# Feed-forward operands of a Hymba-style layer: the low part of each split operand by an accumulating DMA in place of a VectorE subtraction

## The chip, the cores and the metric

The kernel runs on one core of a Trainium2 chip. The metric is the device time of one execution in microseconds (us), the median over several runs. The engines of the core are PE (TensorE), DVE (VectorE), ACT (ScalarE), POOL (GpSimd) and SP (SyncE). Transfers run on 16 DMA engines that all queues share; before the change every transfer that matters here is issued by SP.

## The reference

One post-norm layer for 1024 positions of width 1024. A mixer (state-space group, retention group, output projection) is followed by a layer norm, and then by the part that the change touches:

```python
def conv_ffn(x, w_up, conv_w, conv_b, w_down):
    ug = x @ w_up                       # 1024 x 5632
    a, g = ug[..., :D_FF], ug[..., D_FF:]          # D_FF = 2816
    a_pad = jnp.pad(a, ((0, 0), (CONV_W - 1, 0), (0, 0)))
    a = sum(conv_w[i] * a_pad[:, i:i + seq_len] for i in range(CONV_W)) + conv_b
    return (jax.nn.silu(a) * g) @ w_down           # 1024 x 1024
x = layer_norm(ALPHA * x + ffn, ln2_g, ln2_b)
```

All of it is float32.

## The kernel before

Float32 precision is had from TensorE's float32r products: each operand is split into a high part (the value rounded to float32r) and a low part (value minus high part), and a product is the sum of three matmuls: high by high, high by low, low by high. The function `split` makes the two parts of a 128x512 operand: ScalarE casts the source into the high part (line 913), VectorE subtracts it from the source into the low part (line 914). The parts stand in a ring of 10 slots (`ring`, filled in `up_setup`), reused in turn, so a slot can be filled again when the products of the operand ten splits earlier are through.

Both products of the feed-forward use Strassen-Winograd, seven block products for eight.

*Up projection* (spans from 403 to 823 us of the profile). A loop over 22 blocks f of 128 hidden units. For each f, `up_products` runs seven products of 12 matmuls (A11, S2, S3, S1, A12, A22, S4), then adds, convolution, SiLU and gate; `up_prep(f + 1)` makes the next seven operands, and `up_load(f + 3)` loads weights that far ahead. Four operands are sums made by VectorE in place in the raw weights, and three of these sums overwrite something that an earlier split still reads: line 932 writes `sS[:, 0]`, the source of the S1 split of the block before; line 934 overwrites a11, the source of the A11 split; line 941 overwrites a12, the source of the A12 split. For the first three blocks the A11 split (and for two of them A12) is made early, while the output projection and first layer norm of the mixer still run; that layer norm has steps on POOL (lines 824 and 831).

*Down projection* (823 to 1034 us). Three sweeps over 11 pairs m of hidden blocks; `down_prep` loads and splits four operands for a pair (two of `araw`, which comes back from DRAM, two of the weights `wd`). One step of a pair uses two of the splits, for 12 matmuls; a sweep has 22 such steps and the three sweeps 66. In the third sweep line 1081 overwrites b21 right after its split, and the result is split again. A last sweep takes its operands from `down_prep_last` (lines 1089 and 1090), which has a cast and a subtraction of its own and does not call `split`.

`split` is called 154 times in the up projection (22 by 7) and 132 times in the down projection (33 by 4): 286 times. The instructions of each engine run in a fixed order, which a planner sets when the kernel is built, from its own costs; each engine waits in that order.

Of the kernel before, what the change touches and what calls it, by code (L numbers as in the profile page):

```python
# [31 lines left out]
# columns of the constant pack  # L32
C_COS, C_SIN, C_MASK, C_XI, C_ZETA, C_G128, C_SGN, C_DM, C_MH, C_END = (
    0, 256, 768, 1280, 1284, 1288, 1290, 1292, 1308, 1312)
# columns of the state-space parameter pack
# [37 lines left out]
class Arena:  # L73
    """Hand-placed SBUF: slots of 8 KB a partition, reused in the order in which they are freed."""
# [32 lines left out]
def layer_kernel(ctx, tc, a, out):  # L107
# [11 lines left out]
    kept = {}       # banks that outlive a turn of the rotation  # L119
# [9 lines left out]
    def f32(t):  # L129
        return t.bitcast(F32)  # L130
# [6 lines left out]
    # ------------------------------------------------------------ inputs of the first phase  # L137
    # mixer-phase small pool
# [28 lines left out]
    def load_w(blk, kp):  # L167
        """two k-tiles of one 512-column block of w_in, split into two float32r parts"""
        n = f"wsp{blk}_{kp}"
        if blk == 1:  # L170
            load_x(kp)
        t = A.get([P, 2, 2, 512], F32R, n)
        rs = []
        for q in range(2):
            wr_n[0] += 1
            r = mp.tile([P, 512], F32, tag=f"wraw{wr_n[0] % 3}", name=f"wraw{blk}_{kp}{q}")
            SP.dma_start(r, a["w_in"][blk, :, 2 * kp + q])
            rs.append(r)
            if blk == 1:
                load_xk(2 * kp + q)  # L180
        for q, r in enumerate(rs):
            S.copy(t[:, q, 0], r)
            V.tensor_sub(t[:, q, 1], r, f32(t[:, q, 0]))
            if blk == 1:
                split_xk(2 * kp + q)
        if blk == 1:
            A.free(f"xraw{kp}")
        return t, n

    # ------------------------------------------------------------ input projection  # L190
    def project(blk, lhs, banks, between=None, after=None):
        """psum[j] (j = 0..7) += x-part.T @ w_in block, k outermost; between: small products to run among the first,
        before the last bank is begun"""
        ws = []
        for kp in range(4):
# [17 lines left out]
            if late:  # L213
                if kp == 0:
                    continue
                after()
                bank_n[0] -= 1          # the bank of the small products
                banks[7] = bank("late")
                for k in range(4):
                    wk = ws[k // 2][:, k % 2]  # L220
                    mm3(banks[7], lhs(k, 0, 7), lhs(k, 1, 7), wk[:, 0], wk[:, 1], k == 0, False)
                A.free(f"wsp{blk}_0")
# [10 lines left out]
    # products of zeros while the first loads are under way, to have the tensor engine's clock up when they arrive  # L233
# [7 lines left out]
    # ------------------------------------------------------------ q, k  # L241
# [7 lines left out]
    for b in range(8):  # L249
# [9 lines left out]
        # q carries gamma^(t+1), which the decay masks take back  # L259
# [8 lines left out]
    # ------------------------------------------------------------ u  # L268
# [17 lines left out]
    # ------------------------------------------------------------ state-space parameters  # L286
# [49 lines left out]
    # lam_bar = mag cos + i mag sin;  cos = 1 - 2 sin^2(r/2)  # L336
# [5 lines left out]
    V.scalar_tensor_tensor(nr, cm, -2.0, m1, ALU.mult, ALU.add)      # Re lam_bar - 1  # L342
# [5 lines left out]
    # kappa = (lam_bar - 1) / lam  # L348
# [16 lines left out]
    def cmul(oR, oI, aR, aI, bR, bI, n, tA=tA, tB=tB):  # L365
        """(aR + i aI) * (bR + i bI) on [P, n, 32]; b is one [P, 32] vector"""
        va = lambda t: t.rearrange("p (m g) -> p m g", g=32)
        bb = lambda t: t.unsqueeze(1).broadcast_to([P, n, 32])
        x, y = va(tA[:, :32 * n]), va(tB[:, :32 * n])
        V.tensor_mul(x, va(aR), bb(bR))  # L370
        V.tensor_mul(y, va(aI), bb(bI))
        V.tensor_sub(va(oR), x, y)
        x2, y2 = x, y
        V.tensor_mul(x2, va(aR), bb(bI))
        V.tensor_mul(y2, va(aI), bb(bR))
        V.tensor_add(va(oI), x2, y2)
# [5 lines left out]
    # kappa * Lambda^m  # L382
# [3 lines left out]
    def rev_pow(t, lo):  # L386
        """[P, 16 g, 8 j, 16 c] view of powers 7-j (stored [m, g]) for groups lo.."""
# [15 lines left out]
    # ------------------------------------------------------------ chunk inputs and kernels  # L403
# [10 lines left out]
    # powers of Lambda^8  # L414
# [9 lines left out]
    # signed imaginary parts: coefficient of the swapped copy, for out = [re; im] and its swap  # L424
# [10 lines left out]
    # chunk states V[(ri, s), 0, g, chunk], one chunk late; the second half is for states with re and im swapped  # L435
# [18 lines left out]
    # short kernels K[(7-m, c'), g, c]  # L454
# [25 lines left out]
    # ------------------------------------------------------------ scan over the chunks  # L480
    def swapped(h, j):
        """position j of every super-chunk, re and im swapped"""
# [19 lines left out]
    def scan_carries():  # L502
        # inclusive states at the end of the 16 super-chunks, carried with Lambda^64
# [18 lines left out]
    def scan_correct(car):  # L522
        # states += Lambda^(8 (j+1)) * carry of the super-chunk before
# [18 lines left out]
    # ------------------------------------------------------------ v  # L542
# [9 lines left out]
    # ------------------------------------------------------------ gate  # L552
# [4 lines left out]
    # ------------------------------------------------------------ state-space output  # L557
    # output taps CT[(ri, s), i', g, c] with Lambda^(8-i'); T'[(j, c'), i', g, c]
    UT, CT, TT = [], [], []
    # L1 = [Lr; -Lr], L2 = [-Li; -Li]  # L560
# [45 lines left out]
    # ------------------------------------------------------------ retention  # L606
# [3 lines left out]
    # heads 0, 2 (state rows 0-63) and 1, 3 (rows 64-127) keep to banks of their own  # L610
# [49 lines left out]
    def ret_norm(b):  # L660
        # per-head norm, gate
# [62 lines left out]
    def glu_setup():  # L724
        # GLU weights [P, k, 512]
# [13 lines left out]
    # one part's products fill the waits of the other  # L739
# [14 lines left out]
    # ------------------------------------------------------------ second half of the mixer  # L754
    def load_split(src, n, name, wide):
        """weights [P, 2048] per raw slot -> float32r parts [P, 2, hl, 1024]"""
# [49 lines left out]
    # Strassen-Winograd operands of the transposed x1: halves of d (rows) and of the tokens (columns).  # L806
    # xf[d half, token half] in float32; X[...] = float32r parts (hi, lo) of [P, 4 k, 512 tokens]
# [25 lines left out]
    def layer_norm_far(zz, lnv, pool, after):  # L833
        """as layer_norm for several tiles that are not waited for"""
# [37 lines left out]
    def x1_transpose(i):  # L872
# [13 lines left out]
        if i >= 4:  # L886
            b11, b21, b12, b22 = (xf[k][:, :, cs] for k in ((0, 0), (1, 0), (0, 1), (1, 1)))
            V.tensor_sub(xt3[:, :, cs], b22, b12)        # T3
            V.tensor_sub(b11, b12, b11)                  # T1
            V.tensor_sub(b12, b22, b11)                  # T2  # L890
            V.tensor_sub(b21, b21, b12)                  # -T4

    # ------------------------------------------------------------ up projection, conv, gate
# [15 lines left out]
    def split(src):  # L909
        """the two float32r parts of a [P, 512] operand"""  # L910
# [3 lines left out]
        V.tensor_sub(t[:, 1], src, f32(t[:, 0]))  # L914
# [5 lines left out]
    def up_prep(f, first=True, rest=True):  # L920
        """operands of the seven products, in the order of their use; sums in place where they can be"""
# [8 lines left out]
        if rest:  # L930
            s1 = sS[:, 0]
            V.tensor_add(s1, a21, a22)
            V.tensor_sub(a21, a11, a21)                  # S3
            V.tensor_sub(a11, s1, a11)                   # S2  # L934
# [6 lines left out]
            V.tensor_sub(a12, a12, a11)                  # S4  # L941
# [5 lines left out]
    def ahead(f):  # L947
        """how many of the products of f run before the operands of the others are there"""
# [27 lines left out]
    def up_products(f):  # L976
# [23 lines left out]
        # causal depthwise conv, slots -2, -1 hold the last two positions of the chunk before  # L1000
# [13 lines left out]
    # operands of the down projection made of h (rows: token halves, columns: even and odd f):  # L1014
    # A11, S1, S2, S3, A12, A22, S4 for every pair of f
    hd = dr.tile([NF // 2, P, 7, 512], F32, name="hd")

    def store_h(f):
# [9 lines left out]
        V.tensor_sub(a21, a11, a21)                      # S3  # L1028
# [12 lines left out]
    # ------------------------------------------------------------ down projection, second norm  # L1041
    # Strassen-Winograd again: B rows are the even and odd f of each pair, columns the halves of n
# [8 lines left out]
    def down_load(s_, m):  # L1051
        """loads of pair m for one sweep"""
# [13 lines left out]
    def down_prep(s_, m):  # L1066
        """operands of pair m for one sweep; sums of the weights in place"""
        r = down_load(s_, m)
        b11, b12, b21, b22 = wd[m][:, 0, 0], wd[m][:, 0, 1], wd[m][:, 1, 0], wd[m][:, 1, 1]
        if s_ == 0:  # L1070
            ops = [(split(r[:, 0]), split(b11))]
            V.tensor_sub(b12, b12, b11)                  # T1
            ops.append((split(r[:, 1]), split(b12)))
        elif s_ == 1:
            V.tensor_sub(b12, b22, b12)                  # T2
            ops = [(split(r[:, 0]), split(b12))]
            V.tensor_sub(b11, b12, b11)                  # T3
            ops.append((split(r[:, 1]), split(b11)))
        else:
            ops = [(split(r[:, 0]), split(b21))]  # L1080
            V.tensor_sub(b21, b21, b12)                  # -T4  # L1081
# [3 lines left out]
    def down_prep_last(m):  # L1085
        """operands of the last sweep: S4 (which came in the place of T3) and B22"""
# [49 lines left out]
    # in the order of their last use  # L1136
# [7 lines left out]
    def residual():  # L1144
        for e in range(2):
            t = A.get([P, 4, DM], F32, f"zw{e}")
            V.tensor_copy(t[:, 0, 0:1], u[:, e, 0:1])        # holds the load back until the first sweep is through
# [3 lines left out]
    def spread(s_):  # L1151
        """alpha * x1 and what the first two sweeps give, into the quarters of the output (rows: token halves)"""
# [68 lines left out]
def lay_out(i):  # L1221
    """The inputs, rearranged (no arithmetic)."""
# [43 lines left out]
```

## Time and profile before

| | |
|---|---|
| median of 3 runs | 1043.98 us (1043.65 to 1045.77) |
| profiled execution, first to last instruction (span) | 1043.1 us |
| what lies around the span, by the median | 0.9 us |
| busy: PE, DVE, ACT, POOL | 1022.4, 827.7, 455.7, 59.5 us |
| moved by DMA | 122.22 MB, mean 117 GB/s |

For the profiled execution the page gives its span; no separate device time of that one execution stands beside it. Busy time is the time in which an engine has an instruction in work. A wait is idle time of an engine put down to the instruction that released it. The granted clock is a share of TensorE's full 2.4 GHz. The DMA share is the mean busy share of the 16 DMA engines.

### The profile page before, as it was taken

To read this page: it belongs to the slowest core of one execution; us is meant where nothing else is said; L and a number is where in the kernel's file an instruction comes from. 1 tells how busy PE (TensorE), PEld (TensorE's weight loads), DVE (VectorE), ACT (ScalarE), POOL (GpSimd) and SP (SyncE) were. 2 spreads that over 40 slices of the span, in tenths; PEclk is the share of its full clock that TensorE was granted. 3 is DMA by queue.
4 is the path that set the end of the run, shared out by engine and by line. 5 is a ranking of instruction groups with operands and counts; after the bars stand their busy time and mean duration, and the time that the engine had idled before them with its cause. 6 is when DMAs were issued, how large, how long until landed. Compare 5 with 4: busy or idle time off the path is not lost.

```text
span 1043.1 us, 12923 instructions
## 1 busy us (share of the span) xinstructions
PE 1022.4 (98%) x4780; PEld 862.0 (83%) x4780; DVE 827.7 (79%) x1406; ACT 455.7 (44%) x786; POOL 59.5 (6%) x64
## 2 busy tenths in 40 slices
PE   9999999999999998999999999999999999999996
PEld 7899888887899886788888888888888888888885
DVE  5387999966855799999687787787776896749987
ACT  5121663044622255655444444444444545444710
POOL 0000000002100262000000000000000000000003
PEclk9999999999999999999999999999999999999999
DMA  8400401413500422043223233123133895743103
GB/s 287 156 1 1 172 19 43 135 67 122 184 0 23 159 82 101 13 150 140 91 108 115 79 112 142 51 111 142 51 131 126 308 321 208 256 137 125 53 37 125
DMA packets 37263, 122.22 MB, mean 117 GB/s; under 512 B 4192, under 2 KB 6624, under 8 KB 32336
## 3 DMA queue, kind: packets, MB, share of 16 engines
q1 hardware_dynamic: 36912, 120.88, 32.6%
q8 instruction: 37, 0.61, 0.3%
q10 hardware_dynamic: 288, 0.52, 0.1%
q14 instruction: 26, 0.21, 0.1%
HBM read 90.22 MB, written 31.16 MB: 116 GB/s over the span
## 4 chain that ended last, share of the span: by engine, by line
PE 86%; DVE 6%; issue 2%; POOL 2%; ACT 2%; DMA 1%; POOLq 0%; SPq 0%; DVEq 0%; ACTq 0%
PE dn L134 6%; PE dn L135 6%; PE dn L133 6%; PE u L206 4%; PE qk L206 4%; PE g L206 4%; PE wo L133 2%; PE wo L134 2%; PE wo L135 2%; PE o L634 1%; PE v L206 1%; PE o L636 1%; PE y L599 1%; POOL z L831 1%; PE glu L133 1%
## 5 line engine op out<-in xcount | busy, mean ns | idle before, releaser
L913 ACT CAST ring<-wu 128x512 fp32r<-128x512 f32 x132 | 81.4, 620 | 144.0 <-DVE wu L934 6.3
L914 DVE TENSOR_TENSOR ring<-wu,ring 128x512 fp32r<-128x512 f32 x132 | 92.8, 705 | 18.9 <-ACT ring L913 18.9
L133 PE MATMUL dn<-ring 128*128 128x512 f32 x264 | 102.7, 389 | 0.0
L134 PE MATMUL dn<-ring 128*128 128x512 f32 x264 | 102.7, 389 | 0.0
L135 PE MATMUL dn<-ring 128*128 128x512 f32 x264 | 102.7, 389 | 0.0
L913 ACT CAST ring<-araw 128x512 fp32r<-128x512 f32 x66 | 41.1, 623 | 78.2 <-PE dn L134 67.2
L914 DVE TENSOR_TENSOR ring<-araw,ring 128x512 fp32r<-128x512 f32 x66 | 45.6, 691 | 29.6 <-ACT ring L913 29.6
L133 PEld LDWEIGHTS dn<-ring 128*128 128x128 f32 x264 | 49.5, 188 | 10.4
L134 PEld LDWEIGHTS dn<-ring 128*128 128x128 f32 x264 | 49.6, 188 | 10.3
L135 PEld LDWEIGHTS dn<-ring 128*128 128x128 f32 x264 | 49.5, 188 | 10.2
L914 DVE TENSOR_TENSOR ring<-wd,ring 128x512 fp32r<-128x512 f32 x66 | 45.3, 689 | 1.0 <-ACT ring L913 1.0
L913 ACT CAST ring<-wd 128x512 fp32r<-128x512 f32 x66 | 40.7, 618 | 8.4 <-DVE wd L1081 4.4
L206 PE MATMUL u<-wsp,x 128*128 128x512 f32 x168 | 43.8, 417 | 0.0
L206 PE MATMUL v<-wsp,x 128*128 128x512 f32 x147 | 42.5, 410 | 0.4 <-ACT V L452 0.4
L206 PE MATMUL qk<-wsp,x 128*128 128x512 f32 x168 | 40.5, 403 | 1.4 <-ACT x L161 1.4
L206 PEld LDWEIGHTS u<-wsp,x 128*128 128x128 f32 x168 | 41.7, 330 | 0.1
L206 PEld LDWEIGHTS qk<-wsp,x 128*128 128x128 f32 x168 | 32.5, 194 | 9.5 <-ACT x L161 2.7
L206 PE MATMUL g<-wsp,x 128*128 128x512 f32 x168 | 38.5, 390 | 0.0
L206 PEld LDWEIGHTS g<-wsp,x 128*128 128x128 f32 x168 | 31.5, 188 | 6.9 <-ACT vt L548 0.4
L1008 DVE SCALAR_TENSOR_TENSOR cg<-Ab,cv,cg 128x1024 f32<-128x1024 f32 x22 | 28.3, 1285 | 10.6 <-ACT cg L1007 10.6
L1010 ACT ACTIVATE cg<-cg 128x1024 f32<-128x1024 f32 x22 | 23.4, 1062 | 28.8 <-DVE cg L1009 28.8
L843 POOL TENSOR_SCALAR frs<-fmv 128x4 f32<-128x4 f32 x1 | 1.1, 1147 | 604.1 <-DVE fmv L842 604.1
(1154 smaller groups left out, 2820.2 us busy)
## 6 DMA issues: line engine op xcount, KB each, us to landing
wu<-in_w_up_dram SPq DMA_DIRECT2D x22, 1024.0 KB, 5.0
araw<-hd SPq DMA_DIRECT2D x33, 512.0 KB, 3.7
wraw<-in_w_in_dram SPq DMA_DIRECT2D x32, 256.0 KB, 3.4
hd<-cg SPq DMA_DIRECT2D x22, 256.0 KB, 2.0
hd<-cg SPq DMA_DIRECT2D x11, 512.0 KB, 2.6
hd<-sS SPq DMA_DIRECT2D x11, 512.0 KB, 2.8
wd<-in_w_down_dram SPq DMA_DIRECT2D x11, 512.0 KB, 4.4
wd<-in_w_down_dram SPq DMA_DIRECT2D x22, 256.0 KB, 5.2
```

The source lines that it names most:

```text
L133: T.matmul(o, lhsT=lh, rhs=rh, start=first, stop=False)
L134: T.matmul(o, lhsT=lh, rhs=rl, start=False, stop=False)
L135: T.matmul(o, lhsT=ll, rhs=rh, start=False, stop=last)
L206: T.matmul(banks[j], lhsT=lhs(k, xi_, j), rhs=w[:, q, wi_], start=(k == 0 and xi_ == 0 and wi_ == 0), stop=False)
L599: T.matmul(o, lhsT=UT[h][:, gl], rhs=TT[h][:, :, 16 * gl:16 * gl + 16], start=True, stop=False)
L634: T.matmul(ob[h], lhsT=pt[:, e * P:(e + 1) * P], rhs=v_[:, h * P:(h + 1) * P], start=True, stop=(b == 0))
L636: T.matmul(ob[h], lhsT=qk[rows[h], h // 2], rhs=st[rows[h], h // 2], start=False, stop=True)
L831: G.tensor_add(z, z, lnv[:, 1])
L913: S.copy(t[:, 0], src)
L914: V.tensor_sub(t[:, 1], src, f32(t[:, 0]))
L1008: V.scalar_tensor_tensor(c, Af[:, P:P + 1024], cv[:, f, 1:2], c, ALU.mult, ALU.add)
L1010: S.activation(c, c, AF.Silu)
```

## The change

In `split` the VectorE subtraction is taken out. ScalarE writes the negated source, rounded in the same way, into the low part, and an adding DMA issued by GpSimd then adds the source to it in place. All other lines of the diff are comments that are taken out or blank lines.

```diff
     def split(src):
         t = ring[ring_n[0] % len(ring)]
         ring_n[0] += 1
         S.copy(t[:, 0], src)
-        V.tensor_sub(t[:, 1], src, f32(t[:, 0]))
+        S.activation(t[:, 1], src, AF.Copy, scale=-1.0)
+        G.dma_start(out=t[:, 1], in_=src, accum_op=ALU.add)
         return t[:, 0], t[:, 1]
```

Each source is 128 partitions of 512 float32: 256 KB.

## Rows read from the trace of the kernel before

**Rows 1.** The page: busy time, share of the span, number of instructions.

```profile
PE 1022.4 (98%) x4780; PEld 862.0 (83%) x4780; DVE 827.7 (79%) x1406; ACT 455.7 (44%) x786; POOL 59.5 (6%) x64
```

**Rows 2.** Windows: stretch, length, busy of each engine, granted clock, DMA share, GB/s.

```profile
core 0: us, PE busy (x) PEld busy (x) DVE busy (x) ACT busy (x) POOL busy (x), PEclk, DMA share, GB/s
350.00:400.00 50.00, 46.77 (x231) 39.04 (x229) 46.52 (x72) 21.48 (x34) 26.72 (x14) 1.00 0.20 81
...
540.00:580.00 40.00, 40.00 (x178) 33.10 (x178) 31.29 (x44) 19.39 (x34) 0.00 (x0) 1.00 0.28 99
...
823.00:883.00 60.00, 60.00 (x267) 49.67 (x266) 50.82 (x81) 28.66 (x51) 0.00 (x0) 1.00 0.77 265
883.00:943.00 60.00, 60.00 (x266) 49.71 (x265) 37.99 (x61) 26.48 (x48) 0.00 (x0) 1.00 0.57 203
943.00:1003.00 60.00, 60.00 (x266) 49.67 (x266) 56.55 (x95) 33.74 (x59) 0.00 (x0) 1.00 0.22 71
```

**Rows 3.** Waits of PE from 350 us on: in total, times, longest.

```profile
PE x1t L879 <- POOL z L831: 4.4, 1, 4.4
PE up1C L962 <- DVE ring L914: 0.6, 1, 0.6
```

**Rows 4.** Groups by line: the subtraction of split, and its cast.

```profile
L914 DVE TENSOR_TENSOR ring<-wu,ring 128x512 fp32r<-128x512 f32 x132 | 92.8, 705 | 18.9 <-ACT ring L913 18.9
L914 DVE TENSOR_TENSOR ring<-araw,ring 128x512 fp32r<-128x512 f32 x66 | 45.6, 691 | 29.6 <-ACT ring L913 29.6
L914 DVE TENSOR_TENSOR ring<-wd,ring 128x512 fp32r<-128x512 f32 x66 | 45.3, 689 | 1.0 <-ACT ring L913 1.0
...
L914 DVE TENSOR_TENSOR ring<-sS,ring 128x512 fp32r<-128x512 f32 x22 | 15.2, 692 | 0.0
...
L1089 ACT CAST last<-wd 128x512 fp32r<-128x512 f32 x22 | 12.6, 620 | 3.8 <-DVE last L1090 1.6 <-DVE zw L1159 1.6 <-DMA araw<-hd 0.3
```

**Rows 5.** Timeline of ACT, down projection, two steps of many.

```profile
889.53 0.62 ACT L913 CAST ring<-araw 128x512 fp32r<-128x512 f32 x1 [1.58 <-PE dn L134]
890.06 0.61 ACT L913 CAST ring<-wd 128x512 fp32r<-128x512 f32 x1
892.25 0.62 ACT L913 CAST ring<-araw 128x512 fp32r<-128x512 f32 x1 [1.58 <-PE dn L134]
```

**Rows 6.** Groups of ACT: the ACTIVATE of a 128x512 SBUF tile.

```profile
L1007 ACT ACTIVATE cg<-Ab,cv 128x512 f32<-128x512 f32 x19 | 15.4, 812 | 0.0
```

**Rows 7.** DMA of 823 to 1003 us: packets, MB, share of 16 engines.

```profile
q1 hardware_dynamic: 10496, 32.18, 51.9%
```

**Rows 8.** DMA issues, whole kernel: KB each, us from issue to landing.

```profile
araw<-hd SPq DMA_DIRECT2D x33, 512.0 KB, 3.7
...
hd<-cg SPq DMA_DIRECT2D x22, 256.0 KB, 2.0
hd<-cg SPq DMA_DIRECT2D x11, 512.0 KB, 2.6
```

**Rows 9.** Issuing a DMA on SP: ns min/median/max, first and last start.

```profile
L1058 SPq DMA_DIRECT2D araw<-hd x33: 319/320/434, 779.4 to 970.6; - x33
```

**Rows 10.** Groups of POOL in the first layer norm: busy, mean ns.

```profile
L831 POOL TENSOR_TENSOR z<-z,ln 128x1024 f32<-128x1024 f32 x7 | 17.3, 2476 | 8.8 <-ACT z L830 8.8
L824 POOL TENSOR_TENSOR lrsa<-lrsa,mh 128x1 f32<-128x1 f32 x8 | 12.1, 1513 | 27.4 <-DVE lrsa L823 27.4
```

**Rows 11.** Timeline of DVE, one block of the up projection.

```profile
557.92 0.69 DVE L1005 TENSOR_TENSOR Ab<-cg,up7D 128x512 f32<-128x512 f32 x1 [1.43 <-PE up7D L962]
...
562.88 0.69 DVE L932 TENSOR_TENSOR sS<-wu 128x512 f32<-128x512 f32 x1
...
566.49 0.69 DVE L941 TENSOR_TENSOR wu<-wu 128x512 f32<-128x512 f32 x1
...
572.68 0.69 DVE L934 TENSOR_TENSOR wu<-sS,wu 128x512 f32<-128x512 f32 x1
...
576.96 0.69 DVE L1005 TENSOR_TENSOR Ab<-cg,up8D 128x512 f32<-128x512 f32 x1 [1.43 <-PE up8D L962]
```

**Rows 12.** Windows around PE's one long idle time.

```profile
396.00:400.00 4.00, 0.77 (x8) 0.53 (x5) 4.00 (x6) 2.42 (x4) 2.71 (x2) 1.00 0.00 0
400.00:404.00 4.00, 2.79 (x11) 2.59 (x12) 3.18 (x6) 1.58 (x4) 1.16 (x1) 0.58 0.53 161
```

## Prediction

> **What bounds the kernel now.** I read the busy times first: PE is in work for 98% of the span, DVE for 79% [rows 1]. That is an average, so next the windows: from 540 to 580 us, and in each 60 us of the three sweeps of the down projection, PE is busy for the whole stretch at full granted clock, while DVE is busy for 31.29 of 40 us and 37.99 to 56.55 of 60 [rows 2]. Then the waits of PE from 350 us on: two, 5.0 us together, and only 0.6 us of them ended by the subtraction that goes away [rows 3]. So in the feed-forward PE sets the time, DVE's subtractions are hidden behind it, and the most that the change could win is a part of those 5.0 us. What matters is whether the new path still delivers the operands as fast as PE consumes them.
>
> PE's pace: the same DVE addition of two successive blocks starts 19.04 us apart in the up projection (557.92 and 576.96) [rows 11]: 7 products, 2.72 us each. In the down projection the casts of successive steps start 2.72 us apart, and ACT waits for PE to free a ring slot [rows 5]. One step uses two splits.
>
> **Part 1, the subtraction goes.** 286 instructions, 92.8 + 45.6 + 45.3 + 15.2 = 198.9 us of DVE [rows 4]. None of it stands on the path but for the 0.6 us above. Worth 0 to 0.6 us in the steady stages. In the early stretch (350 to 400 us) DVE is busy 46.52 of 50 us [rows 2], but five early splits' relief (five by 0.7 us) meets five DMA issues put into POOL's queue, among the layer norm steps that end PE's 4.4 us wait [rows 3]. At one POOL instruction of 1.51 us each [rows 10] that is up to 7.6 us the other way. Bounds -4.4 and +7.6; I take 0.
>
> **Part 2, ScalarE's second pass.** The negation is a 128x512 pass from SBUF to SBUF. Nearest rows: the cast, 0.62 us long and 0.53 us after the one before it [rows 5], and an ACTIVATE of that size, 0.81 us [rows 6]. Per step of the down projection ACT then has four passes: 4 by 0.53 = 2.1 us, or 2 by 0.53 + 2 by 0.71 (0.81 less the same overlap) = 2.5 us, of 2.72. It fits. Where the 22 casts of the last sweep's operands run [rows 4] in the last 15 or so steps, 1.5 more per step make 2.9 to 3.3 us: 3 to 9 us over, if nothing slower hides it. In the up projection ACT is at 19.39 of 40 us [rows 2], or 9.2 of 19.04; seven passes add 4.4 to 5.7. It fits.
>
> **Part 3, issuing on POOL.** No DMA of POOL is in the trace. Bounds: SP's issue, 0.32 us [rows 9], and POOL's longest instruction nearby, 2.48 us [rows 10]. Two per step must stay under 2.72 us, so the limit is 1.36 us each. I take POOL's shortest layer norm step, 1.51 us [rows 10], as the row of POOL's own that lies between the ends: 3.0 us per step, 0.3 over. In the up projection seven by 1.51 = 10.6 us of 19.04, and even seven by 2.48 = 17.4, fit.
>
> **Part 4, the transfers.** Each split now moves 256 KB, and adding in place means reading two operands and writing one. In 823 to 1003 us the queue moved 32.18 MB in 51.9% of 180 us [rows 7], so 256 KB of loads takes 0.76 us of all 16 engines. Stores out of SBUF are nearer to this traffic: 512 KB lands 0.6 us later than 256 KB [rows 8]. So one pass costs 0.6 to 0.76 us, and with the destination read as well, two passes, 1.2 to 1.52.
>
> The three windows of the down projection already use 0.77, 0.57 and 0.22 of 60 us each [rows 2]: 93.6 us of the DMA engines in 180. Its 132 splits add 79 us (one pass, 0.6), 100 (0.76), 158 (two passes, 1.2) or 201 (1.52). The sums are 173, 194, 252 and 294 us, against 180 of PE's. What is over 180 cannot be hidden, since loads and accumulations share the engines: 0, +14, +72 or +114 us. Each accumulation is hidden only up to (180 - 93.6) / 132 = 0.65 us. I take two passes at the store's price, 1.2 us: +72 us, a step of 252 / 66 = 3.8 us, which covers ACT's 2.1 to 3.3 and POOL's 3.0.
>
> The Trainium skill bears on the two passes: "Collectives: The Full Stack", section "The bandwidth ceiling: the fold count and why AG ≠ RS ≠ AR", says that an add inside the DMA engines costs nothing for the adding, but halves the rate because it needs two source reads. By this rule the sum is the +72 us taken; no row of this trace has an adding transfer to confirm it.
>
> In the up projection the share is 0.28 at 540 us [rows 2], and seven by 1.2 us of 19.04 add 0.44: 0.72, or 0.84 at 1.52. It fits.
>
> **Part 5, latency.** With 10 ring slots a split may begin four steps ahead in the down projection, 10.9 us. It now needs four ACT passes (2.1), an issue (1.5) and a landing of 2.0 to 3.7 us [rows 8]: 5.6 to 7.3. It fits until the landing passes 7.3 us. In the third sweep line 1081 must wait for a landing before its result is split again: two issues, two landings and 3.8 us of ACT and DVE are 10.8 to 14.2 us for five steps, 13.6; at worst 2.6 us over the sweep, and covered by the 3.8 us step. In the up projection the lead is nine products, 24.5 us. There, three sums of DVE per block (932, 934, 941) must wait until a DMA has read their source [rows 11]. Against cast and subtraction, each wait is 0.53 + 1.51 + (2.0 to 3.7) - 0.69 = 3.3 to 5.0 us longer. Behind it in DVE's order stand the additions that free PSUM banks. DVE has 31.29 of 40 us in use [rows 2], 14.9 per block, less seven by 0.7: 10.0 used, 9.0 free. The waits are 10 to 15 us if DVE stands still for all of them; as far as other instructions stand in between they cost nothing. I take 0.
>
> **Sum.** 1043.1 (the profiled span) + 72 = 1115 us, and 0.9 us around the span as in the median: 1116 us.
>
> **The rivals.**
>
> *Hidden, or faster.* If an accumulation holds the DMA engines for under 0.65 us, POOL issues in under 1.36 us and landings stay under 7.3 us, the down projection stays on PE. Then only the early stretch counts: 1038.5 to 1044 if DVE's relief comes through (up to 5.0 us). For it: one pass at the store's price is 0.6 us. Against it: the second read. The skill's page "DMA: Bandwidth & Descriptors", section "Anatomy of one DMA — SWDGE (gpsimd) path", states for a transfer from GpSimd a fixed part of about 2.0 us and the bytes at 436 GB/s, an estimate of 2.6 us for 256 KB: by that rule alone this rival would come true; SP's store of this size lands in 2.0 us [rows 8].
>
> *Mild.* One pass at the load's price (+14), or POOL's 3.0 us per step as the only limit (66 by 0.3 = +20), or ACT's 3 to 9 us in addition: 1047 to 1100.
>
> *POOL bounds.* At 2.48 us an issue, 132 issues are 327 us in 180: +147, 1191 us. It decides above 252 / 132 = 1.9 us an issue. For it: even a 128x1 instruction takes POOL 1.51 us. Against it: SP's 0.32.
>
> *VectorE bounds the up projection.* If DVE stands still for all three waits, 10 to 15 us against 9.0 free, 20 blocks lose 1 to 6 us each: 20 to 120 us beside the 72, 1136 to 1236.
>
> *The clock.* PE would wait 1.1 us in every step. After 4.4 us of idling the granted clock stood at 0.58 in one window of 4 us [rows 12]. If waits as short as these brought it to 1.2 GHz, a step would take 5.4 us: +180, 1224.
>
> **How the numbers follow.** Two passes on the DMA engines (1100 to 1160): 0.45, and it gives the predicted time. POOL, DVE or the clock above that: 0.22. Mild: 0.21. Hidden: 0.12, half faster by over 0.2%, half within it (0.2%, 2 us, is about what a measurement of this kernel tells from no change). So faster 0.06, same 0.06, slower 0.88. The range from 1047 to 1220 leaves out the hidden cases and the far end of the second group. The likeliest case's own range is 1100 to 1160.
>
> **What would show it.** DVE's busy time falls to about 629 us, ACT's rises to about 633. From 823 us on PE should be busy for some 70% of a longer stretch, its waits ended by the DMAs into the ring, with a DMA share near 1, and the up projection still at 19 us a block. If instead the DMA share stays below 0.8 while PE waits, and POOL's issues stand end to end, the issue was the limit; if DVE idles before 932, 934 or 941 and a block takes longer than 19 us, the waits were. I am wrong if PE shows no new waits.

## The result and the profile after

The changed kernel takes 1191.11 us (1187.76 to 1193.82, 4 runs), the kernel before 1044.41 us in the same comparison: a ratio of 1.1398, 95% interval 1.1383 to 1.1414. That is slower, as forecast, but by 147 us in place of 72. One execution below, the first of experiment 3 (the change without its DMA), ran at a granted clock of 0.85 from beginning to end and took 1130.8 us; its time is not compared. Experiments 1, 2 and 4 to 10 are one execution each, experiments 3 and 11 several; each is compared with the kernel before on the same chip.

The page after, its busy times and DMA queues:

```profile
PE 1062.8 (89%) x4780; PEld 874.2 (74%) x4780; DVE 653.5 (55%) x1120; ACT 595.1 (50%) x1072; POOL 304.3 (26%) x350
...
q0 software_dynamic: 41184, 74.99, 36.2%
q1 hardware_dynamic: 36912, 120.88, 28.3%
```

Against [rows 1], DVE lost 286 instructions and 174 us, ACT gained 286 and 139 us: the counts are as predicted, the times less than the 199 and 177 us that the prediction's signs go by. What sets the end is in PE: its idle time rose from 20.7 us (1043.1 - 1022.4) to 126.2 (1189.0 - 1062.8), and its busy time rose by 40.4 us for the same 4780 matmuls. Queue q0 is the new one. It held the 16 engines for 36.2% of 1189.0 us; over 286 transfers that is 1.50 us each.

The windows after, columns as in [rows 2]; the first lies in the up projection, the other three cover the down projection's three sweeps:

```profile
540.00:580.00 40.00, 37.61 (x167) 30.78 (x165) 20.06 (x27) 22.27 (x41) 11.51 (x14) 1.00 0.79 184
...
872.00:962.00 90.00, 66.06 (x255) 49.00 (x254) 25.99 (x37) 46.83 (x86) 35.31 (x42) 0.94 1.09 280
962.00:1058.00 96.00, 70.98 (x278) 53.45 (x276) 9.09 (x16) 51.10 (x95) 37.81 (x44) 0.93 1.09 270
1058.00:1147.00 89.00, 67.21 (x263) 51.86 (x263) 36.11 (x59) 55.19 (x103) 35.76 (x41) 0.92 0.89 180
```

In the sweeps the DMA share is 1.09, 1.09 and 0.89, where [rows 2] had 0.77, 0.57 and 0.22. A share above 1 means that the records count slightly more than the whole, so a price taken from it can be a few per cent too high. PE has work for about 74% of the time; POOL is busy for 40%. In the up projection nothing is full, and yet PE is no longer busy throughout.

The waits of PE after (us in total, times, longest):

```profile
PE dn L134 <- DMA ring<-wd: 68.8, 37, 9.9
PE up15D L961 <- ACT p L990: 4.9, 1, 4.9
PE up5D L961 <- ACT p L990: 3.6, 1, 3.6
PE up21D L961 <- ACT p L990: 2.7, 1, 2.7
...
PE up9D L961 <- ACT p L990: 2.4, 1, 2.4
...
PE x1t L879 <- POOL z L831: 2.3, 1, 2.3
```

So there are two new waits. In the down projection PE waits for the adding DMAs themselves. In the up projection it waits, mostly in every other block, for ScalarE's copy at line 990. (From line 915 on the lines of the changed kernel are one higher than before, and those of the runs in which `split` has a switch four higher: the sum S4 is line 941 before, 942 in the changed kernel and 945 in those runs.) The wait at `x1t`, 4.4 us in [rows 3], is down to 2.3.

From the first matmul of each stage (the starts of the groups of `up0A`, `dn<-ring` and `dn<-last` in each trace) the 145.9 us of the span come apart:

| us | before | after | difference |
|---|---|---|---|
| up to the first product of the up projection | 402.8 | 400.0 | -2.8 |
| up projection | 421.5 | 472.3 | +50.8 |
| three sweeps of the down projection | 179.5 | 275.4 | +95.9 |
| last sweep, norm, stores | 39.3 | 41.3 | +2.0 |

The issue on POOL and the landings after, first the groups of POOL (busy, mean ns), then the DMA issues (KB each, median us to landing):

```profile
L915 POOL DMA_DIRECT2D ring<-wu x132 | 115.3, 929 | 314.3 <-ACT ring L914 128.6 <-DVE cg L997 54.8 <-DVE cg L993 44.8
L915 POOL DMA_DIRECT2D ring<-araw x66 | 59.6, 903 | 106.4 <-ACT ring L914 79.3 <-DMA ring<-wd 9.4 <-DVE cg L1009 7.0
```

```profile
ring<-wu POOLq DMA_DIRECT2D x132, 256.0 KB, 4.2
...
ring<-araw POOLq DMA_DIRECT2D x66, 256.0 KB, 10.0
ring<-wd POOLq DMA_DIRECT2D x66, 256.0 KB, 9.9
```

An issue takes 0.9 us of POOL, between the bounds 0.32 and 2.48 and below the 1.51 taken; two per step fit. A landing takes 4.2 us in the up projection and 10 us in the down projection, against 2.0 to 3.7 us in [rows 8]. The 10 us is a median over two kinds: in the same view of single stretches it is 13 to 15 us in the first two sweeps, where the engines are full, and 5.0 to 5.5 us in the third.

### The profile page after: what moved, and what is told of

Its sections match the earlier page's. It is cut to its first block, busy times and chain, and to the rows that moved or that the text cites. A ratio compares the mean times of both kernels' runs of the same rounds, so it can differ in the third digit from the quotient of the medians.

```text
span 1189.0 us, 13673 instructions
## 1 busy us (share of the span) xinstructions
PE 1062.8 (89%) x4780; PEld 874.2 (74%) x4780; DVE 653.5 (55%) x1120; ACT 595.1 (50%) x1072; POOL 304.3 (26%) x350
## 3 DMA queue, kind: packets, MB, share of 16 engines
q0 software_dynamic: 41184, 74.99, 36.2%
## 4 chain that ended last, share of the span: by engine, by line
PE 34%; DMA 29%; issue 14%; DVE 9%; ACT 7%; POOL 6%; POOLq 0%; SPq 0%; DVEq 0%; ACTq 0%
DMA ring<-wu 9%; DMA ring<-wd 7%; POOL ring L915 5%; DMA ring<-araw 4%; PE u L206 4%; PE qk L206 3%; PE g L206 3%; DMA ring<-sS 3%; DMA araw<-hd 3%; ACT ring L914 2%; PE wo L133 1%; PE wo L134 1%; PE wo L135 1%; DMA wd<-in_w_down_dram 1%; PE wp L135 1%
## 5 line engine op out<-in xcount | busy, mean ns | idle before, releaser
L915 POOL DMA_DIRECT2D ring<-wu x132 | 115.3, 929 | 314.3 <-ACT ring L914 128.6
L134 PE MATMUL dn<-ring 128*128 128x512 f32 x264 | 113.2, 429 | 68.8 <-DMA ring<-wd 68.8
L134 PEld LDWEIGHTS dn<-ring 128*128 128x128 f32 x264 | 52.6, 199 | 95.2 <-DMA ring<-wd 85.0
L133 PE MATMUL dn<-ring 128*128 128x512 f32 x264 | 107.8, 408 | 1.9 <-ACT ring L913 1.5
L135 PE MATMUL dn<-ring 128*128 128x512 f32 x264 | 107.7, 408 | 0.0
L915 POOL DMA_DIRECT2D ring<-araw x66 | 59.6, 903 | 106.4 <-ACT ring L914 79.3
L914 ACT ACTIVATE ring<-wu 128x512 fp32r<-128x512 f32 x132 | 80.8, 626 | 0.0
L915 POOL DMA_DIRECT2D ring<-wd x66 | 58.4, 920 | 70.8 <-ACT ring L914 45.1
L935 DVE TENSOR_TENSOR wu<-sS,wu 128x512 f32<-128x512 f32 x22 | 16.2, 734 | 104.4 <-DMA ring<-wu 104.4
L133 PEld LDWEIGHTS dn<-ring 128*128 128x128 f32 x264 | 52.5, 199 | 15.3 <-ACT ring L913 1.9
L135 PEld LDWEIGHTS dn<-ring 128*128 128x128 f32 x264 | 52.9, 200 | 10.2
L1082 DVE TENSOR_TENSOR wd<-wd 128x512 f32<-128x512 f32 x11 | 7.6, 692 | 95.2 <-issue 67.0
L206 PEld LDWEIGHTS u<-wsp,x 128*128 128x128 f32 x168 | 41.7, 330 | 0.1
L914 ACT ACTIVATE ring<-araw 128x512 fp32r<-128x512 f32 x66 | 41.6, 630 | 0.0
L933 DVE TENSOR_TENSOR sS<-wu 128x512 f32<-128x512 f32 x22 | 15.2, 692 | 47.9 <-DMA ring<-sS 41.6
```

The costliest lines, as they stand in the source:

```text
L133: T.matmul(o, lhsT=lh, rhs=rh, start=first, stop=False)
L134: T.matmul(o, lhsT=lh, rhs=rl, start=False, stop=False)
L135: T.matmul(o, lhsT=ll, rhs=rh, start=False, stop=last)
L206: T.matmul(banks[j], lhsT=lhs(k, xi_, j), rhs=w[:, q, wi_], start=(k == 0 and xi_ == 0 and wi_ == 0), stop=False)
L914: S.activation(t[:, 1], src, AF.Copy, scale=-1.0)
L915: G.dma_start(out=t[:, 1], in_=src, accum_op=ALU.add)
```

## The experiments

All stage times are from the same three first matmuls as in the table above; "up" runs from the first product of the up projection to the first of the down projection.

**1 and 2. One projection at a time.** `split` gets a switch between the two ways; experiment 1 sets it in the up projection only, experiment 2 in the down projection only.

```diff
-    def split(src):
+    def split(src, add=False):
...
         S.copy(t[:, 0], src)
-        S.activation(t[:, 1], src, AF.Copy, scale=-1.0)
-        G.dma_start(out=t[:, 1], in_=src, accum_op=ALU.add)
+        if add:
+            S.activation(t[:, 1], src, AF.Copy, scale=-1.0)
+            G.dma_start(out=t[:, 1], in_=src, accum_op=ALU.add)
+        else:
+            V.tensor_sub(t[:, 1], src, f32(t[:, 0]))
 # 1: up_op calls split(src, True).  2: the default is True, up_op calls split(src, False)
```

> Only the up projection's operands are split by the adding DMA; the down projection subtracts on VectorE as before. Theory A (two separate costs: waits of in-place sums in the up projection, about 48 us; DMA engines full in the down projection, about 96 us): about 1092 us, the down projection back at 180 us with PE busy throughout. Rival (one cost, that of a planner's order or of DMA load carried from one stage into the next): the stages do not come apart, the down projection stays over 200 us or the up projection returns to about 420 us.

> Only the down projection's operands are split by the adding DMA. Theory A: about 1140 us (1044 + 96), up projection as before, DMA share near 1 in the first two sweeps. Rival: well under 96 us, because loads that came late out of the up projection made the rest.

Measured: 1090.2 us with the up projection alone (before, on the same chip: 1045.2), and 1142.0 with the down projection alone. The losses, 45 and 97 us, add up to 142 of the 147. In the first run the sweeps take 179.5 us, as before; in the second the sweeps take 272.9 us and the up projection 422.9. The two costs are separate, and the rival of a cost carried over falls.

**3. ScalarE's second pass without the DMA.**

```diff
         S.activation(t[:, 1], src, AF.Copy, scale=-1.0)
-        G.dma_start(out=t[:, 1], in_=src, accum_op=ALU.add)
```

> The adding DMA is left out; ScalarE's second pass stays, so the low part is the negated source (this changes what is computed). It measures the second pass alone. Theory A: 1044 to 1053 us, nothing but some us in the third sweep, where ScalarE has up to six passes a step. Rival (ScalarE's doubled work is a good part of the loss): over 1065 us.

The same edit, in several executions:

> The adding DMA left out again, ScalarE's second pass kept (the low part is the negated source, which changes what is computed), timed in three rounds, since in the first look the granted clock stood at 0.85 from the first microsecond on and PE waited for nothing. Theory A: 1040 to 1053 us. Rival (ScalarE's doubled work costs time by itself): over 1065 us at full clock.

Measured: 1041.78 us, a ratio to before of 0.9963 (0.9949 to 0.9978). Two windows of that profile, up projection and second sweep:

```profile
460.00:820.00 360.00, 360.00 (x1590) 298.09 (x1589) 202.12 (x263) 239.58 (x418) 0.00 (x0) 1.00 0.30 112
...
880.00:940.00 60.00, 60.00 (x266) 49.69 (x265) 11.07 (x18) 51.10 (x96) 0.00 (x0) 1.00 0.58 205
```

PE is busy throughout, though ACT works 51 of 60 us. The second pass costs nothing, and VectorE's relief is worth about 3 us (2 to 5 by the interval): the first product of the up projection starts at 400.4 us in place of 402.8. The whole loss of the change hangs on the DMA.

**4. The DMA without the addition.** The transfer copies the source over the low part.

```diff
-        G.dma_start(out=t[:, 1], in_=src, accum_op=ALU.add)
+        G.dma_start(out=t[:, 1], in_=src)
```

> The same DMA from GpSimd without the addition: the source is copied over the low part (this changes what is computed); issue, semaphores and waits are the same, one operand is read in place of two. Theory A: engine time per DMA halves to about 0.75 us, the down projection needs 94 + 99 = 193 us (+14) and the up projection keeps most of its loss, since sums still wait for a landing: 1085 to 1105 us. Rival (issue on GpSimd or landing time bounds the down projection): within 20 us of the changed kernel, about 1175 us.

Measured: 1112.1 us, a little over the expected 1105. Its DMA queue (packets, MB, share):

```profile
q0 software_dynamic: 41184, 74.99, 21.4%
```

The same packets and bytes are counted, but 21.4% of 1110.3 us over 286 transfers is 0.83 us each, against 1.50 with the addition: 1.8 times less. The sweeps take 211.6 us in place of 275.4, so two thirds of their loss goes with the addition alone. The number of issues and the places of the waits are the same; an issue does shorten from 0.9 to 0.53 us of POOL, but POOL was busy for only 40% of the sweeps. The sum 93.6 + 132 x 0.83 = 203 us is near it. The up projection stays at 456.1 us, 35 over before, though the engine time fell by nearly half: most of its loss is not one of engine time.

**5. The destination named float32.**

```diff
-        G.dma_start(out=t[:, 1], in_=src, accum_op=ALU.add)
+        G.dma_start(out=f32(t[:, 1]), in_=src, accum_op=ALU.add)
```

> All 286 adding DMAs as in the changed kernel, but with the destination named float32, so that nothing is converted. Theory A (the cost is the second read): 1185 to 1195 us, 1.5 us of the DMA engines each, as before. Rival (the conversion into float32r costs engine time): well under 1.5 us each and under 1150 us.

Measured: 1190.5 us, with the queue's share at 36.2% again. Conversion costs nothing here; the addition does.

**6. Half of the down projection's transfers.** Only the two operands of `araw` in each pair go by the adding DMA.

```diff
-            ops = [(split(r[:, 0]), split(b11))]
+            ops = [(split(r[:, 0], True), split(b11))]
...
-            ops.append((split(r[:, 1]), split(b12)))
+            ops.append((split(r[:, 1], True), split(b12)))
 # likewise for the other two sweeps; the default and up_op are False
```

> In the down projection only the two operands of araw in each pair are split by the adding DMA (66 in place of 132), the rest and the up projection subtract on VectorE. Theory A (DMA engines full, 1.5 us for each addition): 94 + 66 x 1.5 = 193 us in place of 180, so 1057 to 1065 us. Rival (a landing that comes too late for its ring slot, whatever the load): more than half of the 97 us stays, over 1090 us.

Measured: 1059.9 us (before: 1044.6), the sweeps 195.7 us. Windows of the first two sweeps and the third:

```profile
823.00:883.00 60.00, 54.01 (x226) 43.43 (x225) 36.33 (x55) 30.73 (x56) 14.78 (x17) 0.94 1.05 299
883.00:943.00 60.00, 55.26 (x236) 44.92 (x235) 21.29 (x34) 36.80 (x69) 17.39 (x20) 0.97 1.05 299
943.00:1003.00 60.00, 60.00 (x266) 49.71 (x265) 45.96 (x76) 47.87 (x88) 19.16 (x22) 1.00 0.94 212
```

PE waits only where the DMA share is at its ceiling, and not at 0.94. Half the transfers cost 15 us, not half of 97: what counts is the part above what PE's 180 us can hide. In the third sweep this run changes a second thing: the source that line 1081 overwrites is split on VectorE, so that line waits for no landing (see Part 5 below).

**7 and 8. Which operands of the up projection.** Sums made in place overwrite A11, A12 and S1. Experiment 7 splits only the other four by the adding DMA, experiment 8 only these three; the down projection subtracts on VectorE, here and in the rest.

```diff
-        ... in split(src)]
+        ... in split(src, n in ("S2", "S3", "A22", "S4"))]     # 7
+        ... in split(src, n in ("A11", "A12", "S1"))]          # 8
```

> In the up projection only the four operands S2, S3, A22 and S4 are split by the adding DMA, whose sources no later sum overwrites within the block; A11, A12 and S1, which sums overwrite, and the down projection subtract on VectorE. Theory A (the up projection's loss is the in-place sums' wait for a landing): 1042 to 1050 us. Rival (it is the load on the DMA engines and GpSimd): four sevenths of 45, about 1070 us.

> The converse: only A11, A12 and S1 of the up projection are split by the adding DMA. Theory A: most of the 45 us stays though there are fewer transfers, 1075 to 1090 us. Rival (load): three sevenths of 45, about 1063 us.

Measured: 1044.7 and 1066.5 us (before: 1044.6). Four transfers a block cost nothing, three cost 22 us, so it is not load that costs. That rests on experiment 7; the 1066.5 us of experiment 8 alone lie nearer to the rival's 1063 than to the 1075 to 1090 expected. The rest of the 45 us comes only when all seven go that way.

**9 and 10. What line 942 waits for.** All seven operands go by the adding DMA (experiment 1), with one thing undone. In 9 the sum S4 is written over a21, whose split stands two before that of A12, and not over a12, whose transfer has just been issued; in 10 A12 alone is subtracted on VectorE.

```diff
-            V.tensor_sub(a12, a12, a11)
-            up_op(f, "S4", a12)
+            V.tensor_sub(a21, a12, a11)                        # 9
+            up_op(f, "S4", a21)
...
-        ... in split(src, True)]
+        ... in split(src, n != "A12")]                         # 10
```

> The up projection's seven operands by the adding DMA, the down projection by VectorE, as in the run that lost 45 us; but the sum S4 is written over a21, whose split is three older, in place of a12, whose transfer has just been issued. Same transfers, same passes. Theory B (PE waits in the up projection because line 942 waits for the landing of A12, and the copy that frees bank D stands behind the cast of S4 in ScalarE's order): 1042 to 1060 us. Rival (the wait of line 935 for A11, or the load): 25 us or more of the 45 stay, over 1070 us.

> As the run with the whole up projection by the adding DMA, but A12 alone subtracted on VectorE: line 942 has no landing to wait for, six of seven transfers stay. Theory B: 1042 to 1060 us. Rival (line 935 or load): 25 us or more of the 45 stay, over 1070 us.

Measured: 1054.1 and 1045.7 us (before: 1045.2). In 9 the ten blocks from the first product of block 10 to that of block 20 take 190.4 us, and in 10 as well; before it was 190.4, in experiment 1 it was 214.6. What is left of 9's loss lies before block 10, which starts 8.4 us later than before; there PE waits 4.4 us in block 2 and 1.9 us in block 3 for copies of ScalarE. A window of 9 and one of 10, both in the up projection:

```profile
620.00:660.00 40.00, 40.00 (x179) 33.10 (x178) 22.40 (x29) 25.07 (x45) 12.95 (x15) 1.00 0.85 197
```

```profile
620.00:660.00 40.00, 40.00 (x178) 33.10 (x178) 24.77 (x33) 26.39 (x47) 12.75 (x15) 1.00 0.77 184
```

PE is busy for the whole window, with the DMA share at 0.85 and 0.77: above and just below that of the changed kernel's window (0.79), where PE waited. So it is not load: the loss goes when S4's sum no longer depends on the transfer of A12.

The loss does not follow the idle time just before that line. Waits of VectorE for landings (us, times, longest), first in experiment 1 and then in experiment 9:

```profile
DVE wu L938 <- DMA ring<-wu: 104.5, 19, 6.2
DVE sS L936 <- DMA ring<-sS: 41.7, 18, 4.8
DVE wu L945 <- DMA ring<-wu: 7.9, 7, 3.2
```

```profile
DVE wu L938 <- DMA ring<-wu: 78.5, 19, 7.8
DVE wu L945 <- DMA ring<-wu: 22.2, 19, 4.5
DVE sS L936 <- DMA ring<-sS: 8.4, 10, 2.0
```

In 9 line 945 stands idle longer than in experiment 1, and yet the later blocks lose nothing. What differs is when the sum comes. From block 10 on it stands three or seven places behind line 936, the sum that waits for S1's landing, in VectorE's order of experiment 1; in 9 it stands one or two places ahead of that line, in 10 five ahead or right behind. The planner set these orders after the edit, so the runs do not separate the landing of A12 from the place in the order.

**11. A version that might beat before.** Only the five early splits go by the adding DMA, where VectorE is full.

```diff
+        ... in split(src, f < EARLY and (n == "A11" or n == "A12" and ahead(f) == 2))]
```

> Only the five early splits (A11 of blocks 0 to 2, A12 of blocks 0 and 1) go by the adding DMA, all others by VectorE's subtraction. In the changed kernel the first product of the up projection began about 3 us earlier than before. Theory A (that is VectorE's relief in the output projection, where it is full): 1040.5 to 1043 us, faster by 1.5 to 4 us. Rival (the 3 us come from the later splits' absence too, or are lost again before block 3): within 1 us of before.

Measured: a ratio of 1.0001 (0.9991 to 1.001): no gain. In the profile the first product starts at 401.3 us, 1.5 us earlier than before, and the first of the down projection at 823.2 in place of 824.3: about 1 us, too little to be told from no change.

## Why the prediction was right in direction and wrong in size

The prediction forecast +72 us and the runs show +147. 1191 us lies in the stated range only because that range takes in the rivals; the likeliest case's own range ended at 1160. Two terms failed: a wait in the up projection that was put at nothing (Part 5, about 48 us), and the price of a transfer that was taken too low (Part 4; the sweeps lost 96 us in place of 72).

**What bounds the kernel.** Right: PE did before, and with the subtraction gone and nothing in its place that PE waits for (experiment 3) only 3 us can be won, within the 5.0 us of [rows 3].

**Parts 2 and 3.** ScalarE's second pass fits, as forecast (experiment 3). POOL's issue was taken as 1.51 us, over the limit of 1.36; it is 0.9 us and fits. The error did no harm, since the transfers were the larger term.

**Part 4, the transfers: right mechanism, term too small.** The sum of engine time stands for the first two sweeps, where the DMA share is at its ceiling, and for experiment 6 (193 us expected, 195.7 measured): loads and additions share 16 engines, and what is over PE's time shows. The mis-sized term is the price of an addition: 1.2 us, from the increment between two stores in [rows 8], where the run with the down projection alone gives 1.45 us (16.8% of 1140.2 us over 132) and the changed kernel 1.50. The upper end of that term, two passes at the load's price from [rows 7], 1.52 us, was right, and gave +114 where the sweeps show +96. The difference of landing time between two stores was not a measure of engine time; the queue's share was, and it stood in the trace [rows 7]. The rule on two source reads from the Trainium skill ("Collectives: The Full Stack", the section cited ahead) agrees: with the addition 1.50 us, without it 0.83, a factor of 1.8.

**Part 5, the waits: the step that failed.** "As far as other instructions stand in between they cost nothing. I take 0": it was +48 us with the first product's earlier start included. The prediction looked behind lines 932, 934 and 941 in VectorE's order. The queue that mattered was ScalarE's, one step on. Four timelines of the changed kernel show the chain, POOL, DVE, ACT and PE:

```profile
608.03 0.86 POOL L915 DMA_DIRECT2D ring<-wu  x1 [1.41 <-ACT ring L914]
...
610.07 0.69 DVE L933 TENSOR_TENSOR sS<-wu 128x512 f32<-128x512 f32 x1 [2.11 <-DMA ring<-sS]
...
612.25 0.69 DVE L942 TENSOR_TENSOR wu<-wu 128x512 f32<-128x512 f32 x1 [0.16 <-DMA ring<-wu]
...
613.03 0.62 ACT L913 CAST ring<-wu 128x512 fp32r<-128x512 f32 x1 [3.78 <-DVE wu L942]
613.56 0.58 ACT L990 COPY p<-up9D 128x512 f32<-128x512 f32 x1
...
614.19 0.50 PE L961 MATMUL up9D<-XB,ring 128*128 128x512 f32 x1 [2.36 <-ACT p L990]
```

The transfer of A12 is issued at 608.03 and lands at 612.2; line 942, which overwrites its source, has waited for that; ScalarE stood still for 3.78 us before the cast of S4; behind that cast stands the copy of bank D; and PE's next product into bank D waits 2.36 us for the copy. VectorE stood idle only 0.16 us just before line 942, but 2.11 us before line 933, three instructions earlier, for the landing of S1: even without the landing of A12 the sum could have started only 0.16 us earlier in this block, since the landing of S1 held VectorE's order back as well. VectorE had the spare time that the prediction counted, and ScalarE had it too. The chain costs because a short copy that PE needs soon stands in a fixed order behind a cast that waits, over VectorE, for a DMA.

Experiments 9 and 10 show that the loss hangs on the dependence of line 942 on the transfer of A12: without it the blocks take their 19.04 us again. How much of it is the landing of A12 itself, and how much the place behind line 933 that the planner gave the sum, was not separated. The wait of line 935 (934 before), 104.4 us in the changed kernel and still 78.5 and 71.1 us in 9 and 10, costs PE nothing there. The prediction had named the sign: VectorE idle before 932, 934 or 941, and a block longer than 19 us.

Why three transferred operands cost 22 us and seven 45 can be read in part. The spans of experiments 1 and 8 differ by 23.8 us: PE idles 51.0 us in the one and 38.1 in the other, and is busy for 1037.4 and 1026.5. So about half is idle time, with waits of 2.4 us in most of these blocks against 1.7, and the rest goes with the lower clock after them (last section). Line 936 waits 41.7 us for the landing of S1 in experiment 1 and 1.4 us in experiment 8. Which of the four added transfers makes the waits longer is open.

**Part 5, the third sweep.** The prediction took the wait of line 1081 (1082 after) for the landing of b21 as covered by a step of 3.8 us. The third sweep takes 88.0 us (59.8 before), 4.0 us a step, where the engine time comes to 13 + 44 x 1.50 = 79 us; line 1082 stands idle 28.2 us in it for landings, and PE 21.6 us. Lines of DVE, POOL and ACT in it:

```profile
1094.43 0.69 DVE L1082 TENSOR_TENSOR wd<-wd 128x512 f32<-128x512 f32 x1 [4.25 <-DMA ring<-wd]
...
1102.30 0.69 DVE L1082 TENSOR_TENSOR wd<-wd 128x512 f32<-128x512 f32 x1 [2.60 <-DMA ring<-wd]
...
1096.60 1.75 POOL L915 DMA_DIRECT2D ring<-wd  x2 [4.88 <-ACT ring L914]
...
1103.03 0.62 ACT L913 CAST ring<-wd 128x512 fp32r<-128x512 f32 x1 [2.58 <-DVE wd L1082]
```

This reads as a circle: two transfers are issued from 1096.60 on, line 1082 waits for a landing until 1102.30, ScalarE's cast waits for line 1082, and the next issue, at 1104.48, waits for ScalarE. One turn takes 7.87 us, and PE needs 5.44 us for the two steps of a pair. The DMA share from 1092 to 1112 us is 1.01, near the ceiling of 1.09, so load has a part in the landing time. No run undoes this wait alone; what share of the third sweep's 28 us it makes is not shown. So the nearness of +114 to +96 in Part 4 may be in part luck.

**The rivals.** "Hidden" fell on the second read, as argued; even the plain copy's 0.83 us is over its limit of 0.65. "POOL bounds" gave the right total, 1191 us, by luck: POOL was busy for 26% of the span. "VectorE bounds the up projection" was near in price (20 to 120 us), but what PE waited for was ScalarE's copy. The lower end of the first rival, 1038.5 us, comes out as 1039 by its own terms (1044 less 5.0). The Trainium skill ("DMA: Bandwidth & Descriptors", section "Anatomy of one DMA — SWDGE (gpsimd) path") led to an estimate of 2.6 us for a transfer of 256 KB from GpSimd. The plain copies of experiment 4 land in 2.7 to 3.0 us in the third sweep, near that estimate; the adding transfers land in 4.2 us in the up projection and 13 to 15 us under a full load.

**The clock.** It did not fall for whole stages, but it fell after some of the waits (last section).

## What to carry to other kernels

An addition inside a DMA is not free because an engine is relieved of it: weigh its engine time, here 1.8 times that of a copy, against what the DMA engines have left in that stage, and take the price from a queue's share in the trace and not from landing times. Where a source is handed to a DMA, look for the next instruction that overwrites it, and then follow the wait over two engines: look at what stands in fixed order behind the instruction that waits for the waiting one. Writing a sum over a buffer whose reader is older, at no cost in memory, took 36 of the 45 us back (experiment 9).

## What the runs showed of the hardware

After a wait of 2.4 us PE ran for a while at its lower level, 1.2 GHz, with a delay. PE after, behind the wait that ends at 614.19:

```profile
614.52 0.40 PE L962 MATMUL up9D<-XB,ring 128*128 128x512 f32 x1
...
616.19 0.63 PE L962 MATMUL up9D<-XB,ring 128*128 128x512 f32 x1
616.62 0.63 PE L963 MATMUL up9D<-XB,ring 128*128 128x512 f32 x1
```

The matmuls after the wait first start 0.23 us apart, and from 615.77 on 0.43 us apart; the granted clock of 612 to 618 us was 0.80. So the waits cost PE more than their own length: in the run with the up projection alone its idle time rose by 30.3 us (51.0 against 20.7) and its busy time for the same matmuls by 15.0 us (1037.4 against 1022.4), a third of the 45 us. The short waits of experiment 8, 1.7 us, left the granted clock of 600 to 640 us at 1.00.
